# The last feed-forward with activations as the stationary operand of its second product

## The chip, the core and the metric

The kernel runs on one core of a Trainium2 chip. The metric is the time of one execution on the device in microseconds (us). Three executions of the kernel before took 1204.53, 1206.55 and 1206.81 us, so the median is 1206.55 us.

## What is computed

Two layers on 512 tokens of 1024 channels. The first mixes with a state-space model, the second with attention over shared latent keys and values. Each mixer and each feed-forward is followed by a layer norm over a scaled residual. Only the last feed-forward and its norm matter here:

```
def sq_relu_mlp(h, w1, w2):            # w1: [1024, 4096], w2: [4096, 1024]
    return jnp.square(jax.nn.relu(h @ w1)) @ w2
...
h = layer_norm(DN_ALPHA * h + sq_relu_mlp(h, w_ff1[1], w_ff2[1]), ln_ffn_g[1], ln_ffn_b[1])
return h
```

## The kernel before

All activations stand with channels on the 128 partitions and the 512 tokens along the free dimension, in 8 tiles of 128x512. Every float32 product is made of three float32r products: each operand is split into a high and a low part, and `mm3` (L571) issues high by high, high by low and low by high. The three lines L573, L574 and L575 are nearly all of the tensor engine's (PE's) work. The first argument of a product after the output is the stationary operand, loaded into the array, and the second is the moving one; in the profile a product is named `ps<-moving,stationary`.

**Weights** come in units of 1 MB (128x2048). `unit(i)` (L548) makes sure that units up to i+3 are loaded and units up to i+1 are split, and hands out unit i. A load (L520, SP's queue) goes to one of two raw buffers. A split is one cast on ACT (L530, `whi`) and two subtractions of half a unit each on DVE (L532, `wlo`). A raw buffer is free for the next load when its subtractions are done. There are four pairs of buffers for split units.

**The feed-forward** (`feed_forward`, L778) goes over the 4096 hidden channels in four quarters, q = 0 to 3. In a quarter, four units of w1 give 8 hidden tiles (`hidden`, L769: relu and square on ACT, square and the low part on DVE), then four units of w2 give this quarter's share of all 8 output tiles. A unit is 2 x 8 x 3 = 48 products of 512 columns. In q = 0 `settle` (L785) makes z = ALPHA * h + ps, later it adds ps to z (L790). The stationary operand is always a 128x128 piece of the weights.

**The last four units** of a feed-forward are done in `boundary` (L812) together with the norm, which runs over channels, that is over partitions. All products but those of the first unit are done for half of the tokens at a time (256 columns): first tiles 2 to 7 for tokens 0 to 255 (half A), then the same for the others (half B). While B is computed, A is normed: mean by products with a constant matrix (L657, L659), squares (L668, L670, L673), their sum over partitions by products (L607), the root (L613 to L620), its spreading over partitions by products with a diagonal matrix (L627, L630), then scaling (L697), the bias on ACT (L701) and the output (L703). B's norm follows the last product. For the last norm `follow` is None: nothing comes behind it.

**Order.** Inside a `manual_schedule()` block every engine takes its instructions in the order in which the code issues them. ACT, DVE and SP then wait in that order. `feed_forward` opens one block per quarter, and `boundary` another.

Of the kernel before, what the change touches and what calls it, by code (L numbers as in the profile page):

```python
# [76 lines left out]
class Net:  # L77
# [79 lines left out]
    def s5_tables(self, pool):  # L157
# [44 lines left out]
        # coef = (a - 1) / lam  # L202
# [11 lines left out]
    def s5_powers(self, pool, i, j):  # L214
        """powers of a, and their products with coef, for eighths i to j"""
# [42 lines left out]
    def s5_outer(self, pool, e, dst, n, t_re, t_im, i, sign):  # L258
        """three operations, to be issued in turn"""
# [9 lines left out]
    def s5_phase(self, e):  # L269
        """the phase of k chunks, in turns"""  # L270
# [20 lines left out]
    def s5_w(self, pool, e):  # L291
        """W: response of the state to an input"""
# [5 lines left out]
    def s5_p(self, e):  # L298
        """P = (a W)^T of every group"""
# [10 lines left out]
    def s5_s(self, e):  # L310
        """inputs of the chunks"""
# [7 lines left out]
    # states before every chunk: a real recurrence in the rotating frame  # L319
# [41 lines left out]
    def s5_q(self, pool, e):  # L361
        """Q: response to the state before a chunk"""
# [6 lines left out]
    def s5_t(self, e):  # L369
        """TT: response within a chunk, with the skip on its diagonal"""  # L370
# [18 lines left out]
    def s5_y(self, e):  # L389
        """outputs, in rows (position, channel)"""  # L390
# [9 lines left out]
    def s5_gelu(self, e):  # L400
        """their gelu, in rows (channel, group) by way of DRAM"""
# [12 lines left out]
    def warm(self, out, n, src=None):  # L414
        """products that nothing reads, while there is nothing else: the tensor engine's clock is halved after a pause"""
# [7 lines left out]
    def s5(self, pool, u0, early):  # L423
        """returns the split gelu'd outputs and the sums of the first units of the glu over them, but the last"""
# [22 lines left out]
        def partial(n):  # L447
            """some products of the glu that are ready"""
# [103 lines left out]
    # the second part of a split can be put off, for the vector engine not to wait  # L552
# [24 lines left out]
    def dense_steps(self, ps, w, col, act, tok=slice(0, T), n=None):  # L577
        """ps [128, tokens] = w[:, :, col].T @ act, over the k tiles of act; stops after every one"""
# [20 lines left out]
    def rstd(self, out, sq, n, eps_col):  # L599
        """sq: tiles [128, tokens] of squares, still to be summed over the partitions; n: their number; stops after the sums and before  # L600
        their spreading"""
# [13 lines left out]
        # the mean of s / var and 1 / s, for a root s that is nearly right  # L615
# [17 lines left out]
    class Norm:  # L633
        """z: 8 tiles [128, T] of the channels, normed in place, then split into act or stored to out"""
        def __init__(self, net, z, act, half, g, b, out=None):
            self.net, self.z, self.act, self.half, self.g, self.b, self.out = net, z, act, half, g, b, out
# [3 lines left out]
        def add(self, j):  # L640
            """z[j] is there"""
# [7 lines left out]
        def mean(self, last=None):  # L649
            """last: a tile that is not in the sum yet"""  # L650
# [3 lines left out]
            if self.out is not None:  # L654
                self.rs = net.psum()[:, 0:T // 2]
# [5 lines left out]
        def squares(self, parts=(0,)):  # L661
            """z less its mean, and its squares, summed over the tiles from every one of parts to the next"""
# [22 lines left out]
        def finish(self):  # L685
            """stops after every tile"""
# [8 lines left out]
            for j in range(NT):  # L695
                zj = self.z[j][:, c]
                v.scalar_tensor_tensor(zj, zj, g[:, j:j + 1], self.rs, op0=ALU.mult, op1=ALU.mult)  # L697
                if self.out is not None:
                    if j % 2 == 0:
                        pair = net.f("o").rearrange("p (j t) -> p j t", j=2)  # L700
                    act.activation(pair[:, j % 2, :], zj, AF.Identity, bias=b[:, j:j + 1])  # L701
                    if j % 2:
                        net.nc.sync.dma_start(out=self.out[j - 1:j + 1, :, c].rearrange("j p t -> p j t"), in_=pair)  # L703
                    yield
                    continue
# [4 lines left out]
            if self.out is None:  # L710
                lo(NT - 1)
                yield

        def keep(self):
            """the normed z itself, for the next residual; stops after every tile"""
# [5 lines left out]
    def rms_norm(self, x, g, n):  # L721
        """x: tiles in PSUM [128, T]; the split normed tiles, with the tokens put in order; stops after every tile,
        after the sums, before and after their spreading"""
# [26 lines left out]
    # tokens of layer 0 stand in the order (position in a chunk, chunk)  # L750
# [10 lines left out]
    class Ahead:  # L761
        """the first three units of the next layer"""
# [15 lines left out]
    def feed_forward(self, u0, h, act, hid, g, b, follow=None, out=None, aside=iter(())):  # L778
        """hid: the hidden tiles of the first three units; aside: work for the vector engine that fits in"""
        v = self.nc.vector  # L780
        z = [None] * NT
        for q in range(4):
# [26 lines left out]
            if q == 3:  # L809
                return z, self.boundary(u + 4, hid, settle, z, g, b, follow, out)  # L810

    def boundary(self, u, src, settle, z, g, b, follow=None, out=None, pool=None, begun=None):  # L812
        """the last four units before a layer norm, the norm, and the first three after it: half of the tokens is
        normed while the other is computed"""
        nc = self.nc
        tokA, tokB = self.HALVES
        act = [] if out is not None else [tuple(self.f(n, pool=pool or self.A, dt=F32R) for n in ("hh", "hl"))
                                          for _ in range(NT)]
        A, B = [self.Norm(self, z, act, i, g, b, out) for i in range(2)]
# [24 lines left out]
        with self.tc.manual_schedule():  # L844
# [31 lines left out]
            if follow:  # L876
                self.ahead(follow.u + 4, follow.u + 2)
# [4 lines left out]
            if not follow:  # L882
                self.later = None
                put(B, 2)
                go(fin, 4)
                put(B, 1)
                put()
                B.mean(NT - 1)
                go(fin, 2)
                B.squares((0, 1, 2, 3, 4, 5))  # L890
                B.sums()
                go(fin)
                B.root()
                B.spread()
                go(B.finish())
                return act
# [4 lines left out]
            def run2(i, tok, ms=(0, 1)):  # L901
                """both tiles of a unit in turn, for its rows may still be on their way"""
# [42 lines left out]
    def project(self, u0, act, h, g, b, follow, order=None, zpool=None, pool=None, begun=None):  # L945
        """layer norm of ALPHA * h + act @ w, for a [DM, DM] matrix in four units"""
# [12 lines left out]
        return z, self.boundary(u0, act, settle, z, g, b, follow, None, pool, begun)  # L959
# [19 lines left out]
    def rope(self, x, then):  # L979
        """x [128, T]: two heads of 64 rows; rotated in place"""  # L980
# [78 lines left out]
    def values(self, p, a):  # L1059
        """two of the four token tiles, for both heads"""  # L1060
# [12 lines left out]
    def query_rope(self, p):  # L1073
        """rotary parts of both heads, scaled"""
# [26 lines left out]
    def scores(self, hd, t):  # L1101
        """exponentials of the scores of query tile t [128 queries, keys up to them]"""
# [22 lines left out]
    def transposed(self, hd, t):  # L1125
        """into room for the two parts of p^T of one head: key tile k has the queries from 128 k on"""
# [15 lines left out]
    def attention(self, u0, latent, kvg, qg):  # L1142
# [10 lines left out]
        def fill(steps):  # L1153
            """products of the next layer's first unit with the heads that are there"""
# [11 lines left out]
        def ahead(p, s):  # L1166
            """what the coming queries need, some of it for the next two heads"""
# [62 lines left out]
def net_kernel(ctx, tc, a):  # L1230
# [7 lines left out]
    for name, cnt in UNITS.items():  # L1238
        at[name] = len(units)
        for i in range(cnt):  # L1240
            u = a[name][i] if name != "att" else a[name + "qk"[i % 2]][i // 2]
            units.append((u.rearrange("p k n -> p (k n)"), u.shape[1:], i % 4 == 3 and name != "att"))
# [42 lines left out]
    n.feed_forward(at["ff1"], h, act, hid, ln[1][2], ln[1][3], None, a["out"])  # L1285


def host_s5(x, lam_re, lam_im, log_dt, b_re, b_im, c_re, c_im, d):
    """layout only"""
# [16 lines left out]
def layout(x, positions, ln_mix_g, ln_mix_b, ln_ffn_g, ln_ffn_b, w_ff1, w_ff2, ssm_lam_re, ssm_lam_im, ssm_log_dt,  # L1306
# [10 lines left out]
    def cut(w, cols):  # L1317
        """[K, N] -> [units, 128, K / 128, cols]"""
# [40 lines left out]
```

## Time and profile before

| what | value |
|---|---|
| median of three runs | 1206.55 us |
| span of the profiled execution, first to last instruction | 1203.0 us |
| PE busy in it | 1171.5 us (97%) |
| DVE busy | 693.1 us (58%) |
| ACT busy | 510.2 us (42%) |
| mean granted clock of PE | 0.993 |

The profile gives the span of the execution that it recorded, and no other time of that one. "Busy" for PE is time in which a product is in its pipeline, and records of neighbouring products overlap; what a product costs is the distance from its start to the start of the next.

### The profile page before, as it was taken

To read this page: it belongs to the slowest core of one execution; us is meant where nothing else is said; L and a number is where in the kernel's file an instruction comes from. 1 tells how busy PE (TensorE), PEld (TensorE's weight loads), DVE (VectorE), ACT (ScalarE), POOL (GpSimd) and SP (SyncE) were. 2 spreads that over 40 slices of the span, in tenths; PEclk is the share of its full clock that TensorE was granted. 3 is DMA by queue.
4 is the path that set the end of the run, shared out by engine and by line. 5 is a ranking of instruction groups with operands and counts; after the bars stand their busy time and mean duration, and the time that the engine had idled before them with its cause. 6 is when DMAs were issued, how large, how long until landed. Compare 5 with 4: busy or idle time off the path is not lost.

```text
span 1203.0 us, 16076 instructions
## 1 busy us (share of the span) xinstructions
PE 1171.5 (97%) x6634; PEld 1002.4 (83%) x6634; DVE 693.1 (58%) x1244; ACT 510.2 (42%) x867; POOL 2.6 (0%) x12
## 2 busy tenths in 40 slices
PE   5899999999999999999999999999999999999996
PEld 3778888999888888888999788889988888888896
DVE  8999552487444434425585787768733442533456
ACT  4888551337314414213356566534731421322324
POOL 0000000000000000000000000000000000000000
PEclk9999999999999999999999999999999999999998
DMA  4122361214232222323311112221322222331212
GB/s 166 47 89 95 97 205 66 96 45 133 72 120 70 105 105 70 105 105 105 127 35 38 43 51 71 71 72 57 119 70 105 73 103 105 105 105 70 105 36 71
DMA packets 28905, 106.16 MB, mean 88 GB/s; under 512 B 10624, under 2 KB 12800, under 8 KB 18208
## 3 DMA queue, kind: packets, MB, share of 16 engines
q1 hardware_dynamic: 27680, 103.04, 25.1%
q10 hardware_dynamic: 1152, 2.10, 0.5%
q8 instruction: 52, 0.85, 0.3%
q14 instruction: 21, 0.17, 0.0%
HBM read 100.93 MB, written 4.19 MB: 87 GB/s over the span
## 4 chain that ended last, share of the span: by engine, by line
PE 91%; DVE 6%; ACT 2%; issue 1%; DMA 0%; ACTq 0%; DVEq 0%
PE ps L574 27%; PE ps L575 27%; PE ps L573 27%; PE ps L397 1%; PE ps L396 1%; PE ps L315 1%; PE ps L1110 1%; PE ps L380 1%; PE ps L1136 1%; PE ps L607 1%; PE ps L1111 1%; PE ps L352 1%; DVE tmpw L264 1%; PE ps L630 1%; PE ps L330 0%
## 5 line engine op out<-in xcount | busy, mean ns | idle before, releaser
L573 PE MATMUL ps<-hh,whi 128*128 128x512 f32 (+1 forms) x704 | 245.0, 348 | 0.0
L574 PE MATMUL ps<-hl,whi 128*128 128x512 f32 (+1 forms) x704 | 243.7, 346 | 0.0
L575 PE MATMUL ps<-hh,wlo 128*128 128x512 f32 (+1 forms) x704 | 243.6, 346 | 0.0
L530 ACT CAST whi<-raw 128x2048 fp32r<-128x2048 f32 (+1 forms) x91 | 165.9, 1834 | 162.7 <-DMA raw<-in_ff 141.6
L532 DVE TENSOR_TENSOR wlo<-raw,whi 128x1024 fp32r<-128x1024 f32 (+2 forms) x182 | 206.4, 1176 | 30.6 <-ACT whi L530 28.6
L573 PE MATMUL ps<-fh,whi 128*128 128x512 f32 (+1 forms) x608 | 216.8, 357 | 0.0
L574 PE MATMUL ps<-fl,whi 128*128 128x512 f32 (+1 forms) x608 | 216.1, 355 | 0.0
L575 PE MATMUL ps<-fh,wlo 128*128 128x512 f32 (+1 forms) x608 | 216.1, 355 | 0.0
L772 ACT ACTIVATE relu<-ps 128x512 f32<-128x512 f32 x64 | 38.1, 595 | 265.8 <-PE ps L575 265.8
L573 PEld LDWEIGHTS ps<-hh,whi 128*128 128x128 f32 x704 | 133.6, 190 | 16.4
L574 PEld LDWEIGHTS ps<-hl,whi 128*128 128x128 f32 x704 | 133.7, 190 | 16.2
L575 PEld LDWEIGHTS ps<-hh,wlo 128*128 128x128 f32 x704 | 133.7, 190 | 16.1
L774 DVE TENSOR_TENSOR relu<-relu 128x512 f32<-128x512 f32 x64 | 44.2, 690 | 169.2 <-ACT fh L773 169.2
L573 PEld LDWEIGHTS ps<-fh,whi 128*128 128x128 f32 x608 | 114.9, 189 | 16.5
L574 PEld LDWEIGHTS ps<-fl,whi 128*128 128x128 f32 x608 | 114.9, 189 | 16.3
L575 PEld LDWEIGHTS ps<-fh,wlo 128*128 128x128 f32 x608 | 114.9, 189 | 16.1
L790 DVE TENSOR_TENSOR z<-z,ps 128x512 f32<-128x512 f32 (+1 forms) x60 | 34.7, 579 | 119.8 <-PE ps L575 119.8
L573 PE MATMUL ps<-yh,whi 128*128 128x512 f32 x128 | 52.3, 410 | 0.0
L670 ACT ACTIVATE q<-z 128x256 f32<-128x256 f32 x64 | 25.0, 418 | 59.8 <-DVE z L668 59.8
L575 PE MATMUL ps<-yh,wlo 128*128 128x512 f32 x128 | 49.7, 390 | 0.0
L574 PE MATMUL ps<-yl,whi 128*128 128x512 f32 x128 | 49.7, 390 | 0.0
L775 DVE TENSOR_TENSOR fl<-relu,fh 128x512 fp32r<-128x512 f32 x64 | 44.2, 691 | 2.1
(255 smaller groups left out, 1744.3 us busy)
## 6 DMA issues: line engine op xcount, KB each, us to landing
raw<-in_ff SPq DMA_DIRECT2D x64, 1024.0 KB, 4.8
raw<-in_glu SPq DMA_DIRECT2D x8, 1024.0 KB, 5.1
raw<-in_w_out SPq DMA_DIRECT2D x4, 1024.0 KB, 5.0
raw<-in_wo SPq DMA_DIRECT2D x4, 1024.0 KB, 4.7
raw<-in_kvq SPq DMA_DIRECT2D x3, 1024.0 KB, 4.9
raw<-in_attq SPq DMA_DIRECT2D x4, 576.0 KB, 3.8
bc<-in_s5x SPq DMA_DIRECT2D x8, 256.0 KB, 4.6
u<-in_s5x SPq DMA_DIRECT2D x8, 256.0 KB, 5.1
```

The costliest lines, as they stand in the source:

```text
L264: v.tensor_tensor(o, self.tab[t][:, 0:n, G].rearrange("p m g -> p g m").unsqueeze(3).to_broadcast([128, 8, n, 16]), bc[:, j].unsqueeze(2). ...
L315: self.nc.tensor.matmul(s[:, g * 64:g * 64 + 64], st["P"][g // 4][:, 128 * (g % 4):128 * (g % 4) + 128], st["U"][:, g, :], start=True, sto ...
L530: self.nc.scalar.copy(hi, raw)
L532: self.put_off(lambda c=c: self.nc.vector.tensor_tensor(lo[:, c], raw[:, c], hi[:, c].bitcast(F32), op=ALU.subtract))
L573: pe.matmul(ps, whi, ahi, start=start, stop=False)
L574: pe.matmul(ps, whi, alo, start=False, stop=False)
L575: pe.matmul(ps, wlo, ahi, start=False, stop=stop)
L670: act.activation(qs[j], zj, AF.Square)
L772: self.nc.scalar.activation(r, ps, AF.Relu)
L774: self.nc.vector.tensor_tensor(r, r, r, op=ALU.mult)
L775: self.nc.vector.tensor_tensor(lo, r, hi.bitcast(F32), op=ALU.subtract)
L790: v.tensor_tensor(z[m][:, tok], z[m][:, tok], ps, op=ALU.add)
```

## The change

The diff also drops comments and docstrings, and the branches of `Norm` and `boundary` that served the last norm (no follower). What replaces them:

```
+    def mm3_rows(self, ps, a, tok, w, k, start, stop):
+        pe = self.nc.tensor
+        (ahi, alo), (whi, wlo) = a, w
+        pe.matmul(ps, ahi[:, tok], whi[:, k, :], start=start, stop=False)
+        pe.matmul(ps, alo[:, tok], whi[:, k, :], start=False, stop=False)
+        pe.matmul(ps, ahi[:, tok], wlo[:, k, :], start=False, stop=stop)
+
+    def feed_forward_rows(self, u0, h, act, hid, rows, out):
+        nc, v, pe = self.nc, self.nc.vector, self.nc.tensor
+        toks = [slice(128 * t, 128 * t + 128) for t in range(4)]
+        z = [[None, None] for _ in toks]
+        gb = []
+        for i in range(2):
+            for n in range(2):
+                r = self.f("gb", pool=self.B)
+                nc.sync.dma_start(out=r, in_=rows[i:i + 1, 512 * n:512 * n + 512].to_broadcast([128, 512]))
+                gb.append(r)
+        g, b = gb[0:2], gb[2:4]
+
+        def turned():
+            for n in range(2):
+                for t, tok in enumerate(toks):
+                    ps = self.psum()
+                    for j in range(4):
+                        pe.transpose(ps[:, 128 * j:128 * j + 128], h[4 * n + j][:, tok], self.ident)
+                    z[t][n] = self.f("z", pool=self.A)
+                    nc.scalar.mul(z[t][n], ps, ALPHA)
+                    yield
+
+        def settle(t, n, ps):
+            v.tensor_tensor(z[t][n], z[t][n], ps, op=ALU.add)
+
+        def norm(t):
+            st = stats[t]
+            mu, var, s, y, r = [st[:, i:i + 1] for i in (12, 13, 14, 15, 0)]
+            v.bn_aggr(st[:, 12:14], st[:, 0:12])
+            v.tensor_scalar(var, var, self.col(6), None, op0=ALU.add)
+            nc.scalar.activation(s, var, AF.Sqrt)
+            v.reciprocal(y, var)
+            v.scalar_tensor_tensor(z[t][0], z[t][0], mu, g[0], op0=ALU.subtract, op1=ALU.mult)
+            v.scalar_tensor_tensor(y, s, 0.5, y, op0=ALU.mult, op1=ALU.mult)
+            v.reciprocal(r, s)
+            v.scalar_tensor_tensor(y, r, 0.5, y, op0=ALU.mult, op1=ALU.add)
+            for n in range(2):
+                if n:
+                    v.scalar_tensor_tensor(z[t][n], z[t][n], mu, g[n], op0=ALU.subtract, op1=ALU.mult)
+                o = self.f("o")
+                v.scalar_tensor_tensor(o, z[t][n], y, b[n], op0=ALU.mult, op1=ALU.add)
+                nc.sync.dma_start(out=out[toks[t], 512 * n:512 * n + 512], in_=o)
+
+        stats = []
+        with self.tc.manual_schedule():
+            turn = turned()
+            for q in range(4):
+                u = u0 + 8 * q
+                last = q == 3
+                for i in range(3 if q == 0 else 0, 4):
+                    w = self.unit(u + i)
+                    for j in range(2):
+                        ps = self.psum()
+                        self.dense(ps, w, slice(128 * j, 128 * j + 128), act)
+                        hid.append(self.hidden(ps))
+                        for _ in range(2):
+                            next(turn, None)
+                    if last and i >= 2:
+                        self.ahead(u + i + 5, u + i + 3)
+                if last:
+                    break
+                for n in range(2):
+                    ps = [self.psum() for _ in toks]
+                    for c in range(2):
+                        w = self.unit(u + 4 + 2 * n + c)
+                        for t, tok in enumerate(toks):
+                            for k in range(4):
+                                self.mm3_rows(ps[t], hid[4 * c + k], tok, w, k, c == k == 0, c == 1 and k == 3)
+                            if c:
+                                settle(t, n, ps[t])
+                        if q == 0:
+                            for _ in range(2):
+                                next(turn, None)
+                hid = []
+            ...
+            nc.scalar.activation(pre, hid[-1][0][:, 0:1].bitcast(F32), AF.Sqrt, bias=self.col(6), scale=0.0)
+            ws = [[None, None], [None, None]]
+            for ts in ((0, 1), (2,), (3,)):
+                for n in range(2):
+                    for t in ts:
+                        ps = self.psum()
+                        for c in range(2):
+                            if ws[n][c] is None:
+                                ws[n][c] = self.unit(u + 4 + 2 * n + c)
+                            for k in range(4):
+                                self.mm3_rows(ps, hid[4 * c + k], toks[t], ws[n][c], k, c == k == 0, c == 1 and k == 3)
+                        ...
+                        settle(t, n, ps)
+                        v.bn_stats(stats[t][:, 6 * n:6 * n + 6], z[t][n])
+                        if n:
+                            norm(t)
```

The call at L1285 becomes `n.feed_forward_rows(at["ff1"], h, act, hid, a["lnr"], a["out"])`. Units of w2 of this layer are laid out as 4 tiles of 128 rows by 512 output channels (shape (4, 512)) in place of 8 by 256, still 1 MB. Gains and biases of the last norm are a new input of two rows (`lnr`). The output is [512, 1024], rows of tokens.

## Rows read from the trace of the kernel before

**Rows 1.** The page's part 4: the chain that ended last, by engine

```profile
PE 91%; DVE 6%; ACT 2%; issue 1%; DMA 0%; ACTq 0%; DVEq 0%
```

**Rows 2.** Windows: length, then busy time (x instructions) by engine, PEclk, DMA, GB/s

```profile
868.00:1140.00 272.00, 272.00 (x1203) 225.36 (x1203) 110.90 (x129) 77.42 (x78) 0.00 (x0) 1.00 0.27 95
```

**Rows 3.** Timeline of PE: start, duration of a record, line, shapes; last second product

```profile
1140.46 0.39 PE L573 MATMUL ps<-fh,whi 128*128 128x512 f32 x1
...
1151.34 0.28 PE L573 MATMUL ps<-fh,whi 128*128 128x256 f32 x1
...
1187.17 0.59 PE L657 MATMUL ps<-s,c 128*128 128x256 f32 x2
```

**Rows 4.** Chain in order of time (start, length): the norm's products for half A

```profile
1170.21 0.43 PE ps L657 x2
...
1177.83 0.34 PE ps L607 x4
...
1180.78 0.44 PE ps L630 x4
```

**Rows 5.** The same chain, its last piece

```profile
1199.55 0.40 ACTq L1354
```

**Rows 6.** Timeline of PE in attention: weights moving, activations stationary

```profile
745.02 0.28 PE L574 MATMUL ps<-wlo,ch 128*128 128x256 f32 x1
745.14 0.28 PE L575 MATMUL ps<-whi,cl 128*128 128x256 f32 x1
```

**Rows 7.** Timeline of PE around transposes, in the mixer and in attention

```profile
109.52 1.04 PE L304 MATMUL ps<-c,W 128*128 128x128 f32 x8
110.40 1.02 PE L352 MATMUL ps<-hs,c 128*128 128x512 f32 x2
...
748.84 0.48 PE L573 MATMUL ps<-ch,whi 128*128 128x512 f32 x1
749.16 0.40 PE L574 MATMUL ps<-cl,whi 128*128 128x512 f32 x1
```

**Rows 8.** Groups of PE by shape, 20 to 126 us: busy, mean ns, idle before

```profile
L304 PE MATMUL ps<-c,W 128*128 128x128 f32 x64 | 8.4, 274 | 2.0 <-DVE W L294 2.0
```

**Rows 9.** Timeline of ACT, where the last second product begins

```profile
1142.15 3.71 ACT L530 CAST whi<-raw 128x2048 fp32r<-128x2048 f32 x2
```

**Rows 10.** Timeline of DVE in the same stretch; in brackets the idle time before

```profile
1144.09 2.36 DVE L532 TENSOR_TENSOR wlo<-raw,whi 128x1024 fp32r<-128x1024 f32 x2 [0.72 <-ACT whi L530]
...
1151.54 0.69 DVE L790 TENSOR_TENSOR z<-z,ps 128x512 f32<-128x512 f32 x1 [4.49 <-PE ps L575]
```

**Rows 11.** Groups of DVE by shape, whole span: busy, mean ns, idle before

```profile
L341 DVE TENSOR_TENSOR_SCAN ga<-D,ps 128x512 f32<-128x512 f32 x8 | 9.7, 1217 | 4.5 <-PE ps L331 4.5
L1114 DVE TENSOR_REDUCE sst<-ps 128x1 f32<-128x512 f32 x8 | 5.5, 686 | 8.9 <-PE ps L1111 8.9
L127 DVE SCALAR_TENSOR_TENSOR r<-pos,r 128x512 f32<-128x512 f32 x3 | 2.1, 685 | 0.0
L1123 DVE TENSOR_SCALAR p<-p,sst 128x512 f32<-128x512 f32 x8 | 3.9, 487 | 0.3
```

**Rows 12.** Timeline of DVE: the short steps of the last root

```profile
1194.10 0.16 DVE L619 RECIPROCAL st<-st 128x2 f32<-128x2 f32 x1
1194.29 0.16 DVE L620 SCALAR_TENSOR_TENSOR st<-st 128x2 f32<-128x2 f32 x1
```

**Rows 13.** Timeline of SP: two weight loads before the quarter q = 0

```profile
859.15 6.41 SPq L520 DMA_DIRECT2D raw<-in_ff  x2
```

**Rows 14.** Timeline of ACT: the cast of the first of these two units

```profile
880.70 1.90 ACT L530 CAST whi<-raw 128x2048 fp32r<-128x2048 f32 x1
```

**Rows 15.** DMA issues: x count, KB each, median us to landing

```profile
pos<-in_pos SPq DMA_DIRECT2D x1, 256.0 KB, 6.5
```

**Rows 16.** Windows (columns as in the second group), around pauses of PE

```profile
48.00:50.00 2.00, 1.06 (x8) 0.86 (x8) 1.97 (x3) 1.49 (x4) 0.00 (x0) 1.00 0.00 0
...
1190.00:1194.00 4.00, 2.88 (x22) 2.71 (x21) 3.34 (x10) 2.83 (x9) 0.00 (x0) 0.84 0.20 66
```

More of the change, by code (lines that the diff above doesn't have):

```diff
@@ L633, with __init__ @@
     class Norm:
-        def __init__(self, net, z, act, half, g, b, out=None):
-            self.net, self.z, self.act, self.half, self.g, self.b, self.out = net, z, act, half, g, b, out
+        def __init__(self, net, z, act, half, g, b):
+            self.net, self.z, self.act, self.half, self.g, self.b = net, z, act, half, g, b
             self.c = net.HALVES[half]
@@ L653, in mean @@
             self.mu, self.rs = ps[:, 0:T // 2], ps[:, T // 2:T]
-            if self.out is not None:
-                self.rs = net.psum()[:, 0:T // 2]
             w = net.c[:, C_MEAN:C_MEAN + 128]
@@ L697, in finish @@
                 v.scalar_tensor_tensor(zj, zj, g[:, j:j + 1], self.rs, op0=ALU.mult, op1=ALU.mult)
[L698 to L705, printed above, removed]
                 act.activation(self.act[j][0][:, c], zj, AF.Identity, bias=b[:, j:j + 1])
@@ L709, in finish @@
                     yield
-            if self.out is None:
-                lo(NT - 1)
-                yield
+            lo(NT - 1)
+            yield
         def keep(self):
@@ L776, in hidden, with feed_forward @@
         return hi, lo
-    def feed_forward(self, u0, h, act, hid, g, b, follow=None, out=None, aside=iter(())):
+    def feed_forward(self, u0, h, act, hid, g, b, follow, aside=iter(())):
         v = self.nc.vector
@@ L809, in feed_forward @@
             if q == 3:
-                return z, self.boundary(u + 4, hid, settle, z, g, b, follow, out)
-    def boundary(self, u, src, settle, z, g, b, follow=None, out=None, pool=None, begun=None):
+                return z, self.boundary(u + 4, hid, settle, z, g, b, follow)
+    def mm3_rows(self, ps, a, tok, w, k, start, stop):
[4 more added lines that the diff above has]
+        pe.matmul(ps, ahi[:, tok], wlo[:, k, :], start=False, stop=stop)
@@ new lines, in feed_forward_rows @@
+    def feed_forward_rows(self, u0, h, act, hid, rows, out):
[17 more added lines that the diff above has]
+                    nc.scalar.mul(z[t][n], ps, ALPHA)
+                    yield
+        def settle(t, n, ps):
[48 more added lines that the diff above has]
+                hid = []
+            self.n += 1
+            pre = self.small.tile([128, 1], F32, tag="pre", name=f"pre{self.n}")
+            nc.scalar.activation(pre, hid[-1][0][:, 0:1].bitcast(F32), AF.Sqrt, bias=self.col(6), scale=0.0)
[9 more added lines that the diff above has]
+                                self.mm3_rows(ps, hid[4 * c + k], toks[t], ws[n][c], k, c == k == 0, c == 1 and k == 3)
+                        if n == 0:
+                            self.n += 1
+                            stats.append(self.small.tile([128, 16], F32, tag="st", name=f"st{self.n}"))
+                        settle(t, n, ps)
+                        v.bn_stats(stats[t][:, 6 * n:6 * n + 6], z[t][n])
+                        if n:
+                            norm(t)
@@ L815, in boundary @@
+    def boundary(self, u, src, settle, z, g, b, follow, pool=None, begun=None):
         nc = self.nc
         tokA, tokB = self.HALVES
-        act = [] if out is not None else [tuple(self.f(n, pool=pool or self.A, dt=F32R) for n in ("hh", "hl"))
-                                          for _ in range(NT)]
-        A, B = [self.Norm(self, z, act, i, g, b, out) for i in range(2)]
+        act = [tuple(self.f(n, pool=pool or self.A, dt=F32R) for n in ("hh", "hl")) for _ in range(NT)]
+        A, B = [self.Norm(self, z, act, i, g, b) for i in range(2)]
@@ L875, in boundary @@
             self.later = []
-            if follow:
-                self.ahead(follow.u + 4, follow.u + 2)
+            self.ahead(follow.u + 4, follow.u + 2)
             go(steps, 7)
@@ L881, in boundary @@
             fin = A.finish()
[L882 to L896, printed above, removed]
             go(fin, 6)
@@ L957, in settle @@
             self.nc.vector.scalar_tensor_tensor(zm, hm, ALPHA, ps, op0=ALU.mult, op1=ALU.add)
-        return z, self.boundary(u0, act, settle, z, g, b, follow, None, pool, begun)
+        return z, self.boundary(u0, act, settle, z, g, b, follow, pool, begun)
     def glu_out(self, pg, pv):
@@ L1241, in net_kernel @@
             u = a[name][i] if name != "att" else a[name + "qk"[i % 2]][i // 2]
-            units.append((u.rearrange("p k n -> p (k n)"), u.shape[1:], i % 4 == 3 and name != "att"))
+            shape = (4, 512) if name == "ff1" and i % 8 > 3 else u.shape[1:]
+            units.append((u.rearrange("p k n -> p (k n)"), shape, i % 4 == 3 and name != "att"))
     n.weights(units)
@@ L1284, in net_kernel @@
     h, act = n.project(at["wo"], o, h, ln[1][0], ln[1][1], first_hidden(at["ff1"], hid), natural, n.B, n.B, begun)
-    n.feed_forward(at["ff1"], h, act, hid, ln[1][2], ln[1][3], None, a["out"])
+    n.feed_forward_rows(at["ff1"], h, act, hid, a["lnr"], a["out"])
 def host_s5(x, lam_re, lam_im, log_dt, b_re, b_im, c_re, c_im, d):
@@ L1323, in ff @@
         w1 = cut(w_ff1[l], 256).reshape(4, 4, 128, 8, 256)
-        w2 = np.stack([cut(w_ff2[l][1024 * q:1024 * q + 1024], 256) for q in range(4)])
+        w2 = [w_ff2[l][1024 * q:1024 * q + 1024] for q in range(4)]
+        if l == 0:
+            w2 = np.stack([cut(w, 256) for w in w2])
+        else:
+            w2 = np.stack([w.reshape(2, 4, 128, 2, 512).transpose(3, 0, 2, 1, 4).reshape(4, 128, 8, 256) for w in w2])
         return np.concatenate([w1, w2], 1).reshape(32, 128, 8, 256)
@@ L1339, in layout @@
         glu=np.concatenate([val, gate], 3), w_out=cut(ssm_w_out[0], 256), ff0=ff(0), kvq=cut(kvq, 256),
-        attk=attk, attq=attq, wo=cut(attn_w_o[0], 256), ff1=ff(1))
+        attk=attk, attq=attq, wo=cut(attn_w_o[0], 256), ff1=ff(1), lnr=np.stack([ln_ffn_g[1], ln_ffn_b[1]]))
     return {k: np.ascontiguousarray(v) for k, v in r.items()}
@@ L1352 @@
         args[name] = nc.dram_tensor(f"in_{name}", a.shape, mybir.dt.from_np(a.dtype), kind="ExternalInput").ap()
-    args["out"] = nc.dram_tensor("out_0", (NT, 128, T), F32, kind="ExternalOutput").ap()
+    args["out"] = nc.dram_tensor("out_0", (T, DM), F32, kind="ExternalOutput").ap()
     with tile.TileContext(nc) as tc:
@@ L1357 @@
     got = r.results[0]["out_0"]
-    return np.ascontiguousarray(got.reshape(DM, T).T).reshape(1, T, DM)
+    return np.ascontiguousarray(got).reshape(1, T, DM)
```

## The prediction

> **What bounds the kernel now.** I read the chain that ended last first: 91% of it is PE [rows 1]. Then the windows: from 868 to 1140 us, nearly all of the last feed-forward, PE has no gap and full clock, while DVE and ACT are busy for 111 and 77 of 272 us [rows 2]. So in the body of this stage only PE's work counts, and whatever DVE or ACT gain or lose there is hidden. Then the timeline of PE in the last second product, which starts at S = 1140.46 and ends at 1187.17, where the norm's L657 begins [rows 3]: 46.71 us. From there to the end of the span (1203.0) 15.83 us pass in which the products are over and half B is normed. The change touches these two stretches, and adds work to PE in the quarter q = 0.
>
> **The price of a product.** From 1140.46 to 1151.34 lie the first unit's 48 products of 512 columns [rows 3]: 10.88 / 48 = 0.2267 us each. The half-wide ones number 6 tiles x 8 k x 3 x 2 halves = 288. Between 1151.34 and 1187.17 PE also does A's L657, L607 and L630: 0.43 + 0.34 + 0.44 = 1.21 us [rows 4]. So 288 products take 35.83 - 1.21 = 34.62, or 0.120 each: two halves cost 0.240, a whole one 0.2267. Swapping the operands should not alter that: in attention, where weights move and activations stand, 256-column products also start 0.12 apart [rows 6].
>
> **The change, part by part.**
>
> (1) Quarters 0 to 2: the second product keeps 192 products of 512 columns in units of 48. Splits are issued one unit ahead as before, and the late hidden tiles are needed a unit later than now. DVE's additions are as many. Zero, covered by the slack in [rows 2].
>
> (2) Transposes: 32 of 128x128 in q = 0, in four batches of eight, all on PE. A batch of eight in a stream of products takes 110.40 - 109.52 = 0.88 us; the first product after transposes is followed after 0.32 us in place of 0.2267, so 0.09 more [rows 7]. 4 x 0.97 = 3.9 us, all on the path. Bounds: without the refill 3.5; with every transpose at the length of its own record, 0.274 [rows 8], 32 x 0.274 = 8.8. I take 3.9, since the distance between starts is what a stream pays.
> ACT's eight scalings of the result, four of them ahead of the cast of the next unit, are of 128x512, 0.6 us each (a cast of four times that takes 1.9 [rows 14], so a quarter of it and some start-up), in a stage where ACT sits idle for 195 of 272 us [rows 2]: zero.
> The Trainium skill (TensorE: Matmul & The Clock Gate, Part 4: PE-mode transpose) speaks against this step: it gives about 275 ns for a transpose within a kernel and says that transposes don't count as activity for the clock. By its figure the step would cost an estimated 8.8 us. The trace agrees with 275 ns as the length of a record, not as the distance between starts.
>
> The eight stores of 256 KB stay eight, on an SP queue with nothing left behind them: zero but for the last, in part 6.
>
> (3) Gain and bias: four loads of 256 KB on SP's queue ahead of q = 0. The nearest load is the broadcast of positions, 6.5 us to landing [rows 15]; four in a row at worst 26 us. What they can delay is the next weight loads. Two loads are out by 865.6 us [rows 13], but the first of those units is cast only at 880.70 [rows 14]; the second unit comes after it and PE wants it another 20 us later (rest of the first unit before it, then that unit). Hidden in both cases; if that cover were gone, the rest of 26 us would be PE's wait.
>
> (4) The last second product: 192 x 0.2267 = 43.5 us in place of 46.7; the sums of the norm no longer need PE. Gain 3.2 us.
>
> (5) A new wait in it. Now the second w2 unit is needed 48 products after S; after the change 12 products after S, for one token tile runs through both units of a row half. The two added look-ahead calls do not help: `unit` for the next one would have issued these splits at the same place, behind the last hidden tile. In the trace that unit's cast starts at 1142.15 (two merged, 1.86 each) [rows 9], and its first subtraction ends at 1144.09 + 1.18 = 1145.27 [rows 10], S + 4.81. PE would want that low part after 14 products, S + 3.17. Wait 1.6 us; the other half is ready at S + 6.0 and then wanted at S + 6.2, no further wait. Bounds: 0 if the cast comes ahead of the last hidden tile's ACT work, 2.9 if two more passes of 128x512, 0.6 to 0.7 us each, stand in front on ACT or DVE. The last unit is the next to be late: its subtractions stand on DVE behind the addition and the statistics of the second token tile. The first two tiles' 48 products end at S + 12.5; 0.2 + 0.69 + 0.69 + 1.18 (part 6 and [rows 10]) make the first subtraction end at S + 15.3, and PE wants it 14 products after 12.5, at S + 15.7. Its raw buffer is free from S + 6.0, some 8 us ahead of that for a load and a cast. Zero, and up to 0.5 with long statistics.
>
> (6) The tail. From the last product's end everything is DVE: addition 0.69 [rows 10], `bn_stats`, then six short steps (aggregation, eps, reciprocal and three for the root), then four passes of 128x512: two centre and scale, two make output. A pass of that form takes 0.69 [rows 11], a short step about 0.2 from start to start [rows 12]. ACT's root hides under the first pass. `bn_stats` isn't in the trace; between a one-operand pass at 0.49 and a scan at 1.22 I take a reduction's 0.69, which also reads one operand of 512 into few numbers [rows 11]. Start of the addition 0.2 after the next product would start: 1151.54 against 1151.34 [rows 3, 10]. Sum: 0.2 + 6 x 0.69 + 6 x 0.2 = 5.5 us. Behind it, as now, the issue, flight and end of the last store: the chain's last ACT work ends at 1199.55 [rows 5], 3.45 before the end. 9.0 us in place of 15.83: gain 6.8. The earlier token tiles' norms, about 5 us each, lie under 10.9 us of products.
>
> **Sum**: -3.2 + 1.6 - 6.8 + 3.9 = -4.5 us. The profiled span is 1203.0, so 1198.5 after; the runs' median stands 3.55 over that span, which I carry over: 1202.0 us, 0.37% less. Bounds of the unknown: `bn_stats` -0.2 to +0.5; transposes -0.4 to +4.9; wait -1.6 to +1.3; last unit +0.5.
>
> **Rivals.**
>
> *Transposes that don't overlap.* If among 512-column products every transpose costs its record of 0.274 us, they take 8.8: 4.9 more, 1206.9 us, no change. Against it: 0.88 for eight in a stream [rows 7]. For it: those streams have other neighbours.
>
> *The clock falls in the last product* (slower). PE pauses for 1.6 us at S + 2.7 and after; if the granted clock went from 2.4 to 1.2 GHz there, every 512-column product would cost 0.2267 more. The gain of 4.5 is lost after 20 such products, and slower by over 0.2% begins at 31 (6.9 us), that is if the clock stays down for some 14 us of the remaining 40; through all 180 it would cost 41 us, 1243. For it: in the tail of before, with PE busy for 2.88 of 4 us in two-column products, it fell to a mean of 0.84 [rows 16]. Against it: around 48 us PE did eight transposes and then nothing for the rest of 2 us, at full clock [rows 16].
>
> *No wait for the second unit.* If the cast of that unit is early after all, 1.6 us more are gained: 1200.4 us. Against it: the order of issue inside one block.
>
> *It does not shorten the tail.* DVE could carry a backlog into the last token tile: one norm, about 5 us, would make the tail 14 us and the time 1207. Against it: the norm before has over 10 us.
>
> **Chances and range.** My forecast with its bounds, including the early cast, 0.76; transposes without overlap or a backlog of DVE, 0.16, at no change; the clock or something like it, 0.08. A measurement of this kernel can tell about 0.2%, 2.4 us, from no change: faster means below 1204.1. The forecast's cases lie there, from 1199.8 (4.5 + 1.6 + 0.2 + 0.4 us gained: early cast, short statistics, no refill) to 1204. The range of 8 in 10 takes in part of the no-change cases: 1199.5 to 1206.0.
>
> **What would show it.** Right: transposes in four batches of just under 1 us; second products 0.2267 apart; one gap of PE of some 1.6 us (perhaps in two parts) about 2.7 us into the last second product, ended by the cast and the subtraction of weights; last product to end of span about 9 us, DVE in a chain without waits. Wrong: a transposed batch of 2 us, a granted clock under 1.00 before the last product, DVE still at an earlier norm when the last product ends, or PE waiting on weights in the first three quarters.

## The result and the profile after

The median of five executions is 1199.43 us (1198.15 to 1199.85) against 1206.55 (1204.49 to 1206.81) before; the ratio is 0.9948 with an interval of 0.9933 to 0.9964. The kernel got faster by 0.5%. The forecast was 1202.0, faster, with 1199.5 as the lower end. The sign came out as forecast and the parts nearly so; the median lies a hair under the range.

The two profiled spans, 1203.0 and 1198.1, differ by 4.9 us, the medians by 7.1. Executions of both kernels fall in groups some 1.6 us apart, for the most part because the tensor engine's clock falls for a few microseconds in some executions and not in others, in a stretch at 650 to 670 us that the change doesn't touch (e5 and last section). So below, stages are compared from a mark behind that stretch: the first mean product of the norm after attention.

The timeline of PE in the kernel before, and then in the changed one: the mark, the first product of the last second product (S) and the last one; before's S and end stand in [rows 3].

```profile
814.40 0.66 PE L657 MATMUL ps<-s,c 128*128 128x256 f32 x2
```

```profile
814.63 0.66 PE L655 MATMUL ps<-s,c 128*128 128x256 f32 x2
...
1144.31 0.39 PE L806 MATMUL ps<-whi,fh 128*128 128x512 f32 x1
...
1189.16 0.39 PE L808 MATMUL ps<-wlo,fh 128*128 128x512 f32 x1
```

The end of the products (E) is 1187.17 before and 1189.16 + 0.23 = 1189.39 after; the spans end at 1203.0 and 1198.1.

| stage | before | after | difference |
|---|---|---|---|
| mark to S (holds the transposes) | 326.06 | 329.68 | +3.6 |
| S to E, last second product | 46.71 | 45.08 | -1.6 |
| E to the end, tail | 15.8 | 8.7 | -7.1 |
| sum | 388.6 | 383.5 | -5.1 |

The traces of e1 and e2 below, the same two kernels again, give every stage of the table again to 0.1 us.

The transposes, in the timeline of PE after; the first of four batches, which all look alike:

```profile
874.15 1.03 PE L829 MATMUL ps<-c,z 128*128 128x128 f32 x8
874.94 0.48 PE L573 MATMUL ps<-hh,whi 128*128 128x512 f32 x1
875.26 0.40 PE L574 MATMUL ps<-hl,whi 128*128 128x512 f32 x1
```

A batch takes 0.79 us, and the product behind it is followed after 0.32 in place of 0.23, as in [rows 7].

All that PE waited for after 820 us, and the place, 12 products behind S:

```profile
PE ps L808 <- DVE wlo L532: 0.5, 1, 0.5
PE ps L806 <- ACT whi L530: 0.4, 1, 0.4
```

```profile
1146.80 0.39 PE L808 MATMUL ps<-wlo,fh 128*128 128x512 f32 x1
1147.63 0.50 PE L806 MATMUL ps<-whi,fh 128*128 128x512 f32 x1 [0.44 <-ACT whi L530]
1147.96 0.40 PE L807 MATMUL ps<-whi,fl 128*128 128x512 f32 x1
1148.89 0.50 PE L808 MATMUL ps<-wlo,fh 128*128 128x512 f32 x1 [0.53 <-DVE wlo L532]
1149.22 0.40 PE L806 MATMUL ps<-whi,fh 128*128 128x512 f32 x1
```

The idle times in brackets count from the end of a record and hide most of the wait. From start to start, the first product behind the gap was due at 1147.03, so the fourth at 1147.71; it begins at 1149.22: 1.5 us lost. The cast and the subtraction that end it, on ACT and DVE, answer to [rows 9, 10]:

```profile
1145.67 1.90 ACT L530 CAST whi<-raw 128x2048 fp32r<-128x2048 f32 x1
```

```profile
1147.61 4.63 DVE L532 TENSOR_TENSOR wlo<-raw,whi 128x1024 fp32r<-128x1024 f32 x4 [0.38 <-ACT whi L530]
```

Windows of the changed kernel (columns as in [rows 2]): PE stays full and at full clock through the body, transposes included, and at full clock through the wait.

```profile
868.00:1144.00 276.00, 276.00 (x1238) 228.98 (x1238) 111.36 (x129) 81.29 (x86) 0.00 (x0) 1.00 0.26 94
...
1144.00:1150.00 6.00, 5.03 (x22) 3.53 (x21) 3.78 (x5) 5.02 (x5) 0.00 (x0) 1.00 0.00 0
```

The old tail handed half of the tokens to and fro between PE, DVE and ACT. Its last passes, from the timelines of DVE and ACT before:

```profile
1196.09 3.22 DVE L697 SCALAR_TENSOR_TENSOR z<-z,vec,ps 128x256 f32<-128x256 f32 x8 [1.31 <-PE ps L630]
```

```profile
1196.61 3.35 ACT L701 ACTIVATE o<-z,vec 128x256 f32<-128x256 f32 x8 [1.66 <-DVE z L697]
```

The tail after is one chain on DVE over a quarter of the tokens, here from its timeline:

```profile
1189.59 0.69 DVE L835 TENSOR_TENSOR z<-z,ps 128x512 f32<-128x512 f32 x1 [4.02 <-PE ps L808]
1190.31 0.69 DVE L905 BATCH_NORM_STATS2 st<-z 128x6 f32<-128x512 f32 x1
1191.04 0.21 DVE L841 BATCH_NORM_AGGREGATE st<-st 128x2 f32<-128x12 f32 x1
...
1191.61 0.73 DVE L845 SCALAR_TENSOR_TENSOR z<-z,st,gb 128x512 f32<-128x512 f32 x1
...
1192.71 0.75 DVE L854 SCALAR_TENSOR_TENSOR o<-z,st,gb 128x512 f32<-128x512 f32 x1
1193.38 0.75 DVE L852 SCALAR_TENSOR_TENSOR z<-z,st,gb 128x512 f32<-128x512 f32 x1
1194.16 0.75 DVE L854 SCALAR_TENSOR_TENSOR o<-z,st,gb 128x512 f32<-128x512 f32 x1
```

It starts 0.2 us behind E, after DVE has idled for 4.02 us, so no backlog reached it, and ends at 1194.91, 3.2 us before the end of the span.

The loads of gain and bias:

```profile
L819 SPq DMA_DIRECT2D gb<-in_lnr x4: 422/440/581, 811.4 to 813.0; - x4
...
DMA to landing us min/median/max: 6.3/6.6/6.7
```

They were issued at 811 to 813 us, 26 us ahead of the next weight load of this trace (839.15), and nobody waited for them.

### The profile page after: what moved, and what is told of

Same layout as the page of the kernel before. It is cut to its first block, busy times and chain, and to the rows that moved or that the text cites. A ratio compares the mean times of both kernels' runs of the same rounds, so it can differ in the third digit from the quotient of the medians.

```text
span 1198.1 us, 15703 instructions
## 1 busy us (share of the span) xinstructions
PE 1167.3 (97%) x6480; PEld 991.9 (83%) x6480; DVE 690.9 (58%) x1220; ACT 501.0 (42%) x843; POOL 2.6 (0%) x12
## 4 chain that ended last, share of the span: by engine, by line
PE 91%; DVE 6%; ACT 2%; issue 1%; DMA 0%; ACTq 0%
PE ps L574 22%; PE ps L575 22%; PE ps L573 22%; PE ps L808 5%; PE ps L807 5%; PE ps L806 5%; PE ps L397 1%; PE ps L396 1%; PE ps L315 1%; PE ps L1190 1%; PE ps L380 1%; PE ps L1216 1%; PE ps L607 1%; PE ps L1191 1%; PE ps L352 1%
## 5 line engine op out<-in xcount | busy, mean ns | idle before, releaser
L573 PE MATMUL ps<-fh,whi 128*128 128x512 f32 (+1 forms) x304 | 108.4, 357 | 0.0
L574 PE MATMUL ps<-fl,whi 128*128 128x512 f32 (+1 forms) x304 | 108.1, 355 | 0.0
L575 PE MATMUL ps<-fh,wlo 128*128 128x512 f32 (+1 forms) x304 | 108.1, 355 | 0.0
L806 PE MATMUL ps<-whi,fh 128*128 128x512 f32 x256 | 100.0, 390 | 0.4 <-ACT whi L530 0.4
L808 PE MATMUL ps<-wlo,fh 128*128 128x512 f32 x256 | 99.7, 390 | 0.5 <-DVE wlo L532 0.5
L807 PE MATMUL ps<-whi,fl 128*128 128x512 f32 x256 | 99.6, 389 | 0.0
L573 PEld LDWEIGHTS ps<-fh,whi 128*128 128x128 f32 x304 | 57.4, 189 | 8.2
L574 PEld LDWEIGHTS ps<-fl,whi 128*128 128x128 f32 x304 | 57.4, 189 | 8.2
L575 PEld LDWEIGHTS ps<-fh,wlo 128*128 128x128 f32 x304 | 57.4, 189 | 8.0
L806 PEld LDWEIGHTS ps<-whi,fh 128*128 128x128 f32 x256 | 48.1, 188 | 10.7 <-ACT whi L530 0.9
```

The source lines that it names most:

```text
L573: pe.matmul(ps, whi, ahi, start=start, stop=False)
L574: pe.matmul(ps, whi, alo, start=False, stop=False)
L575: pe.matmul(ps, wlo, ahi, start=False, stop=stop)
L806: pe.matmul(ps, ahi[:, tok], whi[:, k, :], start=start, stop=False)
L807: pe.matmul(ps, alo[:, tok], whi[:, k, :], start=False, stop=False)
L808: pe.matmul(ps, ahi[:, tok], wlo[:, k, :], start=False, stop=stop)
```

## Experiments

**e1, the kernel before again, and e2, the changed kernel again.** No edit.

> The kernel before, unchanged. Two things are open: the profiled spans differ by 4.9 us (1203.0 and 1198.1), the medians by 7.1. If that is only which of two groups of executions was profiled (a shift of about 2 us that both kernels have), then the executions fall in two groups about 2 us apart, and the last second product starts at another time in the slower group while the tail keeps its 15.8 us. If it is the tail of before, in which PE still works while its clock falls, then the last second product starts at 1140.5 in every execution and the tail is 1 to 2 us longer in some. Median 1206 us either way.

> The changed kernel, unchanged. By the first view (two groups in both kernels) its executions also fall in two groups about 2 us apart, 1198.2 and 1199.7; by the second (the tail of before) they lie within 1 us of each other. Median 1199.4 us.

Seventeen executions of the kernel before, taken beside these: two at 1201.7, five at 1203.2 to 1203.5, six at 1204.6 to 1204.9, four at 1206.3 to 1206.7. e1's own eleven lie in the same four groups, with a median of 1204.47. Six of the changed kernel: two at 1196.6, one at 1198.2, three at 1199.7. In all of them the time is 1.75 to 1.84 us over the span, so the differences lie inside the span, and the mean granted clock falls with them, from 0.996 to 0.991 in the one and from 0.998 to 0.995 in the other. The first view holds, with four groups and three in place of two: both kernels have groups. The profiled execution of e1 took 1204.68 us with a span of 1202.9, so the span of 1203.0 that the prediction worked from does not belong to the median of 1206.55. Matched group by group, lowest with lowest, the change is worth 1201.7 - 1196.6 = 5.1 us, as in the table of stages; the medians' 7.1 and, here, 1204.66 - 1198.93 = 5.7 mix groups. None of the changed kernel's eleven executions lies another 1.6 us up, where four of the seventeen lie; whether the change makes the falls rarer isn't shown.

**e3, no transposes.** The residual's transposition is left out.

```
-                    ps = self.psum()
-                    for j in range(4):
-                        pe.transpose(ps[:, 128 * j:128 * j + 128], h[4 * n + j][:, tok], self.ident)
                     z[t][n] = self.f("z", pool=self.A)
-                    nc.scalar.mul(z[t][n], ps, ALPHA)
+                    nc.scalar.mul(z[t][n], h[4 * n + t], ALPHA)
```

> The changed kernel without the 32 transposes: the residual is taken from the untransposed tiles by the same scaling on ACT, so the transposition of the residual is left out. If the transposes cost PE 0.88 us for each batch of eight: 3.5 us less than the changed kernel, 1195.9 us, the last second product starting 3.5 us earlier. If they cost their records, 0.274 each: 8.8 us less. If PE had slack there: no change.

Median 1196.04 against 1198.93 for e2, again over mixed groups. The mark, S and the last product in its timeline of PE:

```profile
814.43 0.65 PE L655 MATMUL ps<-s,c 128*128 128x256 f32 x2
...
1140.50 0.39 PE L806 MATMUL ps<-whi,fh 128*128 128x512 f32 x1
...
1185.33 0.39 PE L808 MATMUL ps<-wlo,fh 128*128 128x512 f32 x1
```

Mark to S is 326.07, as before the change to 0.01, and 3.6 less than with transposes; the stages behind it keep their 45.1 and, to 0.1, their 8.7. So the transposes cost 3.6 us, 0.11 each, all of it on the path; their records' 0.27 each is refuted. The eight scalings on ACT and the four loads are still there, so these cost nothing.

**e4, the split of the second unit one hidden tile earlier.**

```
-                    if last and i >= 2:
-                        self.ahead(u + i + 5, u + i + 3)
+                        if last and (i, j) in ((2, 1), (3, 0)):
+                            self.ahead(u + i + 5, u + i + 3)
```

> The changed kernel with the split of the second w2 unit of the last quarter issued one hidden tile earlier, so that its cast and subtractions stand ahead of the last hidden tile's work on ACT and DVE. If the wait in the last second product is the order of issue: both pauses of PE there go, 1.5 us less than the changed kernel, 1197.9 us. If the unit's data were late (load or buffer): the pause stays, no change. If the last hidden tile then becomes late: the pause moves to its products, a gain under 1 us.

Its ACT and DVE, and the 13th product behind S = 1142.66:

```profile
1138.59 1.90 ACT L530 CAST whi<-raw 128x2048 fp32r<-128x2048 f32 x1
```

```profile
1140.52 2.36 DVE L532 TENSOR_TENSOR wlo<-raw,whi 128x1024 fp32r<-128x1024 f32 x2 [0.39 <-ACT whi L530]
```

```profile
1142.66 0.39 PE L806 MATMUL ps<-whi,fh 128*128 128x512 f32 x1
...
1145.38 0.39 PE L806 MATMUL ps<-whi,fh 128*128 128x512 f32 x1
...
1185.96 0.39 PE L808 MATMUL ps<-wlo,fh 128*128 128x512 f32 x1
```

Cast and subtractions end at 1142.88, when the last hidden tile's relu begins on ACT (1142.87). The 13th product starts 2.72 behind S, which is 12 x 0.2267, and S to E is 43.5 us, which is 192 x 0.2267: PE no longer waits. The stages gain 1.5 us. The median shows only 0.8 of that (1198.12 against 1198.93, and equal ratios, 0.9952 both), since the step is as long as a group is wide and six executions don't sort it out: the clocks of e4's are 0.993 to 0.997, those of e2's 0.995 to 0.998, so e4's lie a group higher. That is why the next runs fill the pauses first.

**e5 to e7, the pauses at 650 and 659 us filled**, in the kernel before (e5), in the changed one (e6), and in the changed one with e4's edit (e7). The products write a bank that nobody reads.

```
         go(more(3))
+        self.warm(self.psum(), 6)
         next(q)
...
         self.catch_up(3)
+        self.warm(self.psum(), 8)
         next(kv)
```

> The kernel before with products that nothing reads (6 and 8 of 512 columns) in PE's two pauses at about 650 and 659 us, where latents are normed; both kernels have these pauses. If the spread of the executions (1201.7 to 1206.7) comes from the granted clock, which in some executions falls behind a pause there: all executions within 0.6 us of each other, near 1201.7, and a granted clock of 1.00 up to the tail. If the spread comes from elsewhere (start, loads): it stays at 5 us.

> The changed kernel with the same filling. By the sum of the stages (transposes +3.6, last second product -1.6, tail -7.1): 5.1 us less than the kernel before with filling, 1196.6 us, all executions within 0.6 us. If the new pause for the second w2 unit also lets the clock fall in some executions: a second group 1.5 us or more above that.

> The same with the early split as well: 1.5 us less than the changed kernel with filling, 1195.1 us, all executions in one group. If the early split only moved the pause: no difference.

Windows of the kernel before behind the two pauses, and then of e5:

```profile
654.00:656.00 2.00, 2.00 (x12) 2.00 (x11) 0.00 (x0) 1.78 (x3) 0.00 (x0) 0.50 0.00 0
...
664.00:666.00 2.00, 2.00 (x6) 1.62 (x5) 0.68 (x4) 0.69 (x2) 0.00 (x0) 0.50 0.75 217
```

```profile
654.00:656.00 2.00, 2.00 (x20) 2.00 (x19) 0.72 (x3) 1.84 (x3) 0.00 (x0) 1.00 0.00 0
...
664.00:666.00 2.00, 2.00 (x11) 1.64 (x10) 0.00 (x0) 1.62 (x2) 0.00 (x0) 1.00 0.42 168
```

In the stretches where the clock stood at one half it now stands at one. e5: eight of eleven executions at 1202.10 to 1202.14, three at 1203.8 to 1203.9, where unfilled ones spread over 5 us. e6: 1196.83 and 1196.88, one at 1197.33, 1198.48 and 1198.57. e7: four at 1195.29 to 1195.37, one at 1196.89. In none of the three do all lie within 0.6 us, as was expected, but most of the spread was the clock in this place. The fillers have a price: the lowest time rises by 0.5 us in the kernel before (from 1201.61) and by 0.2 in the changed one (from 1196.59). The lowest groups give the change as 1202.1 - 1196.9 = 5.2 us, and the early split another 1.5. The group 1.6 above is not only e6's; in e7 it was the profiled one, and its clock fell around 50 us, in the first stage, as it did in e9's profiled execution:

```profile
50.00:52.00 2.00, 1.56 (x2) 0.84 (x3) 2.00 (x4) 0.83 (x2) 0.00 (x0) 0.54 0.00 0
```

Whether the new wait ever lets the clock fall stays open: no profile caught that.

e7 is the best kernel found: median 1195.33, ratio to the kernel before 0.9925 (0.9913 to 0.9938), against 0.9943 (0.9930 to 0.9957) for e6. The kernel before is the unfilled one there (1204.90); against e5 the change with the early split is worth 6.8 us.

**e8, the plain order in the last quarter.**

```
-            for ts in ((0, 1), (2,), (3,)):
-                for n in range(2):
-                    for t in ts:
-                        ps = self.psum()
-                        for c in range(2):
+            for n in range(2):
+                ps = [self.psum() for _ in toks]
+                for c in range(2):
+                    ws[n][c] = self.unit(u + 4 + 2 * n + c)
+                    for t in range(4):
...
```

> The changed kernel with the last second product in the order of the other quarters: a unit for all four token tiles before the next one. The wait for the second unit goes (1.5 us less), but the four tiles end 2.7 us apart, and DVE needs 5.4 us for each (addition, statistics, norm). If that is so, three tiles of backlog stand behind the last product: tail 8.7 + 3 x 2.7 = 16.8 us and 6.6 us more in all, 1205.5 us. If the norms of the earlier tiles cost the tail nothing: 1.5 us less.

Median 1205.69, no better than the kernel before beside it (1204.90, ratio 1.0007). PE's last product, and DVE's first pass for the third and the fourth token tile and its last pass of all:

```profile
1185.86 0.39 PE L808 MATMUL ps<-wlo,fh 128*128 128x512 f32 x1
```

```profile
1188.61 0.68 DVE L835 TENSOR_TENSOR z<-z,ps 128x512 f32<-128x512 f32 x1
...
1193.84 0.68 DVE L835 TENSOR_TENSOR z<-z,ps 128x512 f32<-128x512 f32 x1
...
1198.42 0.75 DVE L854 SCALAR_TENSOR_TENSOR o<-z,st,gb 128x512 f32<-128x512 f32 x1
```

S to E is 43.5 us, without a wait. But DVE takes 1193.84 - 1188.61 = 5.2 us for a tile, against 2.7 of products, and the fourth tile's addition starts 7.8 us behind E = 1186.09. The tail is 16.2 us, and the stages sum to 5.9 us more than in the changed kernel (6.6 expected). So the norm over rows alone shortens nothing: in the plain order its tail is longer than the old 15.8. It is short because the token tiles are grouped so that only a quarter of the tokens is left behind the last product, and the wait of 1.5 us is the price of that. A norm over partitions with so small a last block was not tried, so what the direction of the norm is worth by itself isn't shown.

**e9, the old tail with fillers** (and e5's edit).

```
+                self.warm(self.psum(), 4)
                 B.squares((0, 1, 2, 3, 4, 5))
                 B.sums()
+                self.warm(self.psum(), 6)
                 go(fin)
```

> The kernel before with the filling of the two pauses and, in its tail, 4 products that nothing reads before B's sums of squares and 6 before the spreading of B's root. If part of the old tail's price is the clock that falls there: the four spreading products take 0.44 us in place of 1.22 and the tail gets about 0.8 us shorter, 15.0 in place of 15.8, so that at most 0.8 of the 7.1 us gained in the tail are clock and the rest is the form of the norm. If the tail is bound by ACT and DVE all through: no change.

Median of eight 1203.14 (1201.47 to 1204.82), 1204.88 for the kernel before beside it. The profiled tail became 1.0 us longer instead, 16.9 against e5's 15.9 from L657 on. Its timeline of PE and a window:

```profile
1192.37 2.91 PE L419 MATMUL ps<-idm 128*128 128x512 f32 x6
1195.07 1.05 PE L630 MATMUL ps<-dg,c 128*128 128x128 f32 x4
```

```profile
1190.00:1193.00 3.00, 2.42 (x15) 2.24 (x15) 2.29 (x7) 1.86 (x6) 0.00 (x0) 0.65 0.00 0
```

The clock had already fallen during the two-column sums, so six fillers took 2.7 us and held up the spreading. The run doesn't answer its question: how much of the old tail's 15.8 us was the clock stays open. Its fastest execution, 1201.47, untraced, is 0.6 under e5's. The rows of the kernel before allow an estimate. In its chain the spreading of B's root is the only work of PE while the clock is down; chain and window:

```profile
1194.83 1.24 PE ps L630 x4
```

```profile
1194.83:1196.05 1.22, 1.22 (x4) 0.93 (x4) 0.00 (x0) 0.12 (x1) 0.00 (x0) 0.50 0.62 209
```

Half A's took 0.44 [rows 4] at full clock, so by this estimate some 0.8 us of the 15.8, and of the 7.1 gained, are the clock.

## Why the prediction was right, and where it was off

- **The bound, and parts 1 and 3**, held: PE is full from 868 to 1144 us, nothing waits in quarters 0 to 2, and the four loads cost nothing (e3), being issued well before anything could wait for them.
- **Part 2, transposes**, was 3.9 and is 3.6 (e3): the 0.88 us for a batch came from one with a product of another kind behind it, and among these products a batch takes 0.79. The rival that each costs its record's 0.274 us fell. The same holds for the rule weighed there (the Trainium skill, TensorE: Matmul & The Clock Gate, Part 4: PE-mode transpose): its 275 ns, which stand there in a sentence on bf16 data, are the length of a float32 record here (0.27), while a transpose adds 0.11 to the path. What it says of transposes and the clock no run here tests: the clock stayed at 1.00 over the stretch with all 32, in batches of 0.8 us between products.
- **Part 4, products**, is exact: without the wait, 43.5 us (e4).
- **Part 5, the wait**, was 1.6 and is 1.5, at the place and by the two causes that were named; e4 shows that it is the order of issue and nothing else. That the size fits so well is in part luck: the cast began at S + 1.36 and not at S + 1.69, because `pre` (L890) now stands behind it, and 0.24 were lost again, 0.1 between the subtraction's end and the product and the rest in restarting. The last unit caused no wait.
- **Part 6, the tail**, was 9.0 and is 8.7. `bn_stats` took the 0.69 that was taken for it, the passes with gain and bias 0.73 to 0.75 instead of 0.69, and the end behind the last pass 3.2 instead of 3.45. The slower passes (+0.2) and short steps that overlap (-0.2) cancel, so DVE's chain fits the forecast 5.5. The rival of a backlog of DVE fell for this order, and e8 shows what it is worth in another. But the 10.9 us of products over each earlier norm hold only for the third token tile; the first two have 5.4 each, and DVE's 5.2 for a tile (e8) fitted in with 0.2 to spare.
- **The rival of the clock** did not occur: in the four profiles that have this wait with nothing else changed in the last quarter (the result's, e2's, e3's and e6's) the clock is 1.00 through it. What was held against it is weak, though: behind the same stretch at 48 us the clock did fall in e7's and e9's profiles. Its price was also too high: where the clock stood at 0.50 in the kernel before, products of 512 columns started 0.43 apart (664.41 and 664.84 us), 0.20 more and not 0.2267.
- **The sum** was -4.5 us and is -5.1 by stages.
- **The step that failed** is the last: the 3.55 us by which the median stood over the profiled span were carried over as if they lay around the span. They don't: every execution stands 1.74 to 1.86 over its own span, and the rest was another group of executions. From 1203.0 + 1.8 = 1204.8 the forecast would have been 1200.3, and with the measured -5.1 it is 1199.7, the group of the changed kernel's profiled execution (1199.85). The median of before stood a group above its profiled execution, that of after in the same group; so some 2 of the 7.1 us between the medians, and with them the side of the range on which the median fell, are as far as is known a matter of which executions were caught. The windows of the clock behind 650 us, which would have told of it, were not read.

## What to carry to other kernels

When a reduction runs across partitions and the result is the last thing computed, swapping the operands of the product before it brings the reduction into rows, and one vector engine's chain on the last quarter of the data can replace a chain over three engines: here 8.7 us for 15.8, of which the small last block is a part that was not measured apart. The price is the transposition of whatever is added in the old layout, and an order in which weights are wanted sooner than the prefetch was built for: move the split, not only the loads. Let the last block of rows be no larger than the vector engine can finish under the next block's products, and compare stages from a mark behind any stretch where the clock varies, before reading a gain of half a per cent from medians.

## What the runs showed of the hardware that was not expected

The granted clock fell behind pauses of PE of only 1.0 to 1.4 us between records, in some executions and not in others. The pauses, in the timelines of PE before and after:

```profile
651.37 1.02 PE L607 MATMUL ps<-c,rq 128*128 128x2 f32 x8 [1.03 <-DVE rq L729]
661.93 1.02 PE L607 MATMUL ps<-c,rq 128*128 128x2 f32 x8 [1.25 <-DVE rq L729]
```

```profile
651.36 1.02 PE L607 MATMUL ps<-c,rq 128*128 128x2 f32 x8 [1.03 <-DVE rq L718]
660.52 1.37 PE L607 MATMUL ps<-c,rq 128*128 128x2 f32 x8 [1.41 <-DVE rq L718]
```

In the kernel before the clock stood at one half (1.2 in place of 2.4 GHz) at 654 to 656 and again at 664 to 666 us, each time about two microseconds behind such a pause. In the profiled execution of the changed kernel, in code that is the same there, it held behind the first pause and fell behind the second; in e2's, the same kernel again, it fell behind both. Windows of the one and then of e2:

```profile
654.00:656.00 2.00, 2.00 (x20) 2.00 (x19) 0.79 (x2) 1.76 (x4) 0.00 (x0) 1.00 0.00 0
...
662.00:664.00 2.00, 2.00 (x5) 1.55 (x6) 1.23 (x7) 0.90 (x3) 0.00 (x0) 0.50 0.33 106
```

```profile
654.00:656.00 2.00, 2.00 (x11) 2.00 (x11) 0.00 (x0) 1.78 (x3) 0.00 (x0) 0.50 0.00 0
...
664.00:666.00 2.00, 2.00 (x6) 1.61 (x5) 0.80 (x5) 0.69 (x2) 0.00 (x0) 0.50 0.67 201
```

A group, some 1.6 us, is as much as the wait in part 5. It need not be one fall: the mark behind the stretch stands at 811.67 in e6, at 814.52 with e2's two falls, and at 814.63 with the single, longer one of the profiled execution. 14 products that nobody reads in the two pauses took most of the falls away (e5): 1202.14 us in the median against 1204.90 for the kernel before beside it, ratio 0.9980 (0.9971 to 0.9989).
